# A hybrid attention and retention block: the order of two copies in a shared PSUM bank, and fewer, pinned requests

## The chip, the cores and the metric

The kernel runs on one core of a Trainium2 chip. A core has five engines that each work through a queue of their own in order: TensorE (PE, matrix products and transposes), VectorE (DVE, elementwise work and reductions), ScalarE (ACT, functions and copies), GpSimd (POOL) and SyncE (SP, which here issues all DMA requests). Data lies in DRAM, in the on-chip SBUF, or in PSUM, eight banks into which PE writes its results. The metric is the device time of one execution in microseconds (us); the kernel before took a median of 2294.67 us in three runs.

## The reference

One decoder block on an input of 1024 tokens by 1024 channels, in float32. A normalised input is projected into queries, keys and values of twelve attention heads, into retention's queries, keys, values and its gate, and into two sigmoid gates. Attention is dilated and windowed, retention is done in chunks of 128 tokens, both are projected and merged, and a squared-ReLU MLP follows:

```python
xn = rmsnorm(x, norm1_g[l])
wl = w_in[l]
qa, ka, va, qr, kr, vr, gr, gate_a, gate_b = [xn @ wl[:, bounds[i]:bounds[i + 1]] for i in range(len(IN_SPLITS))]
qa = rmsnorm(qa.reshape(B, S, ATT_HEADS, ATT_HEAD_DIM), q_norm_g[l])
ka = rmsnorm(ka.reshape(B, S, ATT_HEADS, ATT_HEAD_DIM), k_norm_g[l])
...
for gi, (window, dilation) in enumerate(ATT_GROUPS):        # (128,1), (512,4), (2048,16)
    hs = slice(gi * ATT_HEADS_PER_GROUP, (gi + 1) * ATT_HEADS_PER_GROUP)
    o, lse = dilated_group(qa[:, :, hs], ka[:, :, hs], va[:, :, hs], slopes[hs], window, dilation)
    outs.append(o)
    lses.append(lse)
alpha = jax.nn.softmax(jnp.stack(lses, axis=0), axis=0)
o_a = jnp.sum(alpha[..., None] * jnp.stack(outs, axis=0), axis=0).reshape(B, S, ATT_OUT_W).astype(x.dtype)
o_r = retention(qr, kr, vr)                                 # reshaped by heads
o_r = (head_groupnorm(o_r, ret_gn_g[l], ret_gn_b[l]) * jax.nn.silu(gr.astype(jnp.float32))).astype(x.dtype)
y = jax.nn.sigmoid(gate_a) * (o_a @ w_proj_a[l]) + jax.nn.sigmoid(gate_b) * (o_r @ w_proj_b[l])
x = x + y @ w_out[l]
xn2 = rmsnorm(x, norm2_g[l])
x = x + jnp.square(jax.nn.relu(xn2 @ w_up[l])) @ w_down[l]
```

In `dilated_group` every query block of 128 attends its own block and the one before it: scores plus a linear bias, a softmax, and the sum over the values.

## The kernel before, in words

Large products are done with each float32 operand split in a rounded high part and a rest (`split`: an ACT copy, L330, and a DVE subtraction, L333), and three matmuls (high by high, high by rest, rest by high). The input projection besides saves products in Strassen's manner: a unit of 256 output columns takes seven products (N1 to N7) of 12 large matmuls each. One such product is called a slot. `Pipe` (`pipe`) counts the slots: a function given to `pipe.at(lag, fn)` is run, and its instructions placed, among the matmuls of the slot that comes `lag` slots later; if two functions are due, the first comes after the second of four terms and the other after the third.

The stages are: attention values for all heads (results to DRAM as `v_d`); the input projection of 36 units, of which the first 12 give one head's queries and keys each (scaled roots of their squares to `rs_d`, the rest to `qk_d`, L808); retention in 32 chunks; the projection of attention's output with the first gate; that of retention's output with the second; the output projection; the MLP.

Attention has no stage of its own. Its 96 blocks (12 heads of 8 blocks, in the order of slot and group, strides 4, 8 and 1) are placed from slot 138 of the input projection on, 9 slots to a head. `plan_core` writes them as `events` per slot. With p0 the first slot of head n: `prepare` at p0 - 4 asks for the bias (L679); `bring` at p0 - 4 and at p0 asks for one half of the queries, keys and roots (L697); `scale` multiplies them on DVE two and three slots later (L705); `fetch` asks for one block's values in each slot (L711). A block's work is in `attend`: `scores` in the slot itself (PE, L642; DVE adds the bias and takes the minimum, L645; ACT takes the exponential, L647), and three slots later `turned`, which takes one PSUM bank from the ring `tr` of two. In that bank, columns 0 to 127 receive the output of the block two turns before (`values`: PE, L660; ACT copies it to `acc`, L661; a DMA writes it to DRAM, L662), and the columns behind it receive the transposed probabilities of this block (`turn`: PE, L653; ACT copies them to `pT`, L655). `scores` takes the ring's other bank. The framework makes an engine wait for another one's access to the same PSUM bank whatever the columns.

The order on PE is that of the program. On the other engines and in SP's queue a planner with a cost model places each instruction as early as it thinks its inputs are there; `tc.keep_in_program_order` pins one instruction behind everything that was written before it on its engine. Pools of tiles have a fixed number of buffers: a request or a copy into one waits until the last reader of the buffer's old content is done. `combine` mixes the three groups of a slot's heads; it reads `acc_d` (L446) some slots after the last of the three heads.

Two other places matter here. Between attention and retention, the upper half of the normalised input, kept in DRAM as `xs_d` during attention, is reloaded (L844) and retention's first chunks are asked for (`load_chunk`, L882 and L884). In the two gated projections, gates are loaded (`sg_d`) and put through a sigmoid on ACT at the place of their use (L1034, L1102).

Of the kernel before, what the change touches and what calls it, by code (L numbers as in the profile page):

```python
# [276 lines left out]
def hybrid_block(ctx: ExitStack, tc: tile.TileContext, a: dict, out: bass.AP):  # L277
# [153 lines left out]
    def tokens(rows, g, b):  # L431

        if g == 0:
            return rows[b * P:(b + 1) * P]
        if g == 1:
            return rows[512 * (b % 2):512 * (b % 2) + 512].rearrange("(p r) e -> r p e", r=4)[b // 2]
        return rows.rearrange("(p r) e -> r p e", r=8)[b]

# [186 lines left out]

    def attend(n, b, bias, qk, V, core):
# [6 lines left out]
        acc = core.tile([P, DH + 2], F, name="acc", bufs=7)  # L633

        def scores():
            sp = tr.tile([P, 4, P], F, name="tr")[:, :nk].rearrange("p a b -> p (a b)")
            q = qk[0][b // 4][:, b % 4 * P:b % 4 * P + P]
            at = 0
            for c in range((b + 1 - nk) // 4, b // 4 + 1):
                n0, n1 = max(b + 1 - nk, 4 * c), min(b + 1, 4 * c + 4)  # L640
                to = slice(at, at + (n1 - n0) * P)
                nc.tensor.matmul(sp[:, to], q, qk[1][c][:, (n0 - 4 * c) * P:(n1 - 4 * c) * P], start=True, stop=True)  # L642
                at = to.stop
            s = st["p"] = core.tile([P, 2 * P], F, name="s", bufs=3)
            nc.vector.tensor_tensor_reduce(s[:, :w], sp, bias[:, 2 * P - w:], op0=OP.add, op1=OP.min,  # L645
                                           scale=1.0, scalar=3.0e38, accum_out=acc[:, DH:DH + 1])
            nc.scalar.activation(s[:, :w], s[:, :w], AF.Exp, scale=-1.0, bias=acc[:, DH:DH + 1],  # L647
                                 accum_out=acc[:, DH + 1:DH + 2])

        def turn(bank):  # L650
            tp = bank[:, 1:]
            for j in range(nk):
                nc.tensor.transpose(tp[:, j], st["p"][:, j * P:(j + 1) * P], ident)  # L653
            st["t"] = core.tile([P, 2, P], F, name="pT", bufs=2)
            nc.scalar.activation(st["t"][:, :nk], tp[:, :nk], AF.Copy)  # L655

        def values(bank):
            po = bank[:, 0]
            for j in range(nk):
                nc.tensor.matmul(po, st["t"][:, j], V[b + 1 - nk + j], start=(j == 0), stop=(j == nk - 1))  # L660
            nc.scalar.activation(acc[:, :DH], po, AF.Copy)  # L661
            nc.sync.dma_start(tokens(acc_d[:, h, :], g, b), acc)  # L662

        return scores, turn, values

# [3 lines left out]
    def plan_core():  # L669
# [3 lines left out]
        tiles = {}  # L673

        def prepare(n):

            slot, g = heads[n]
            bias = core.tile([P, 2 * P], F, name="bias", bufs=2)
            nc.sync.dma_start(bias, a["c_bias"][g * SLOTS + slot])  # L679
            tiles[n] = bias, ([], []), {}, {}  # L680

        def bring(n, c):

            slot, g = heads[n]
            r = strides(g)
            for f in range(2):
                x = core.tile([P, 512], F, name="qk"[f] + "T", bufs=2)
                rb = core.tile([P, 512], F, name="rb", bufs=2)
                for j in range(2) if r > 1 else (c,):
                    cs = slice(256 * c, 256 * c + 256) if r > 1 else slice(0, 512)  # L690
                    src = rs_d[4 * n + 2 * f + j, cs]
                    roots = bass.AP(tensor=src.tensor, offset=src.offset, ap=[[0, P], [1, cs.stop - cs.start]])
                    for dst, src in ((x, qk_d[n, f, j][:, cs]), (rb, roots)):
                        if r > 1:
                            dst = dst.rearrange("p (r j i) -> p j r i", r=r // 2, j=2)[:, j]
                            src = src.rearrange("p (r i) -> p r i", r=r // 2)
                        nc.sync.dma_start(dst, src)  # L697
                tiles[n][1][f].append(x)
                tiles[n][2][c, f] = x, rb

        def scale(n, c, f):
            slot, g = heads[n]
            h = g * SLOTS + slot
            x, rb = tiles[n][2].pop((c, f))
            nc.vector.scalar_tensor_tensor(x, x, gqk[:, f, h:h + 1], rb, op0=OP.mult, op1=OP.mult)  # L705

        def fetch(n, b):

            slot, g = heads[n]
            V = tiles[n][3][b] = core.tile([P, DH], F, name="V", bufs=6)  # L710
            nc.sync.dma_start(V, tokens(v_d[n // 4][:, (n % 4) * DH:(n % 4) * DH + DH], g, b))  # L711

        def on(p, fn):
            events.setdefault(p, []).append(fn)

        def begin(n, b):

            bias, qk, _, V = tiles[n]
            stages.append(attend(n, b, bias, qk, V, core))

        stages = []

        def turned(m):

            bank = tr.tile([P, 4, P], F, name="tr")
            if m >= 2:
                stages[m - 2][2](bank)
            if m < len(stages):
                stages[m][1](bank)

        for n in range(HEADS):
            p0 = FIRST + EACH * n
            on(p0 - 4, lambda n=n: prepare(n))
            for c in range(2):
                on(p0 - 4 + 4 * c, lambda n=n, c=c: bring(n, c))
                for f in range(2):
                    on(p0 - 2 + 4 * c + f, lambda n=n, c=c, f=f: scale(n, c, f))
            for b in range(NT):
                p, m = p0 + b, NT * n + b
                on(p, lambda n=n, b=b: fetch(n, b))  # L740
# [6 lines left out]
        for s in range(SLOTS - 1):  # L747
            for i in range(NT // PAIR):
# [7 lines left out]
                for m in range(PAIR + 1):  # L756
                    on(p + 2 + m, lambda held=held: held["parts"].pop(0)())
                on(p + 4 + PAIR, lambda held=held: pipe.at(0, held["parts"].pop(0)))

    with ExitStack() as ph:  # L760
# [8 lines left out]
        def square(n, f, i, sg):  # L769
# [7 lines left out]
            def add():  # L777
# [8 lines left out]
                if sums["n"] == 8 * HEADS:  # L786
# [55 lines left out]
    XS[0, 1] = slot_of(pool(ctx, "x01b", 1))  # L842
    for i, x in enumerate(XS[0, 1]):
        nc.sync.dma_start(x.bitcast(F).rearrange("p a b -> p (a b)"), xs_d[i])  # L844

# [20 lines left out]
    with ExitStack() as ph:  # L866
# [153 lines left out]
    with ExitStack() as ph:  # L1020
        ES, e1, exts = None, ExitStack(), ExitStack()
        OPB = [{"N5": XS[0, 1], "N7": XS[1, 1]}, {}]
        waiting = [("N7", 1)] + [(name, h) for name in ("N1", "N2", "N6") for h in range(2)]
        for n, (d, cs) in enumerate(work):
            if not cs.start:
                ua, = W.take(1)
                uh, ul = W[ua]
            if len(gates) < len(work):
# [4 lines left out]
                           for k in range(SLOTS)], {SLOTS - 1: lambda: W.free(ua)} if cs.start else None)  # L1033
            nc.scalar.activation(gates[n], gates[n], AF.Sigmoid)  # L1034
            nc.vector.tensor_tensor(gates[n], gates[n], pp, op=OP.mult)
# [54 lines left out]
        def result(j, f, cs, src):  # L1090

            n = results.index((j, f, cs.start // 512))
            fetch(n + 2)
            if n not in ahead:
                y = src
# [5 lines left out]
            sgb, y, *pa = ahead.pop(n)  # L1101
            nc.scalar.activation(sgb, sgb, AF.Sigmoid)  # L1102
            if pa:
# [23 lines left out]
        fetch(0)  # L1127
        fetch(1)
        for i, (j, name) in enumerate(order):
            product("pb", j, name, unit, OPB[j // 4], lambda: parts, result)  # L1130
# [404 lines left out]
```

## Time and profile before

| | before |
|---|---|
| median of three runs | 2294.67 us (2290.59 to 2295.46) |
| the profiled execution | 2290.41 us |
| its span, first to last instruction | 2288.6 us |
| granted TensorE clock | 0.994 |
| PE busy | 2196.0 us, 96% |
| DVE, ACT, POOL busy | 61%, 50%, 14% |
| DMA | 359.12 MB, 157 GB/s over the span |

Busy time is the time in which an engine executes instructions. Matmuls are pipelined, so that one is listed with a longer time than the distance to the next one's start. A row of waits names the engine and line that stood idle, what released it, and total us, number of times and the longest. A row of a group or of the order of time names the line, the engine, the operation, what it writes and reads by the program's names, and the shape. A row of a stretch gives its length, then the busy time of PE, weight loads, DVE, ACT and POOL with their instruction counts, the granted clock, the DMA engines' mean share and GB/s.

### The profile page before, as it was taken

Reading aid. Unit: us, or ns where it says so; the run is one execution under the profiler, and the core shown is the slowest. Engines: PE = TensorE matmul, PEld = TensorE weight load, DVE = VectorE, ACT = ScalarE, POOL = GpSimd, SP = SyncE. Lnnn points to the kernel's source line nnn. Section 1 sums busy time; section 2 is a strip of 40 time slices with the busy share of each in tenths; the row PEclk is TensorE's granted clock in tenths of the full one; section 3 lists DMA queues with packets and bytes.
Section 4 is the critical chain, followed back from the end, with each engine's and each line's share of the span. In section 5 each row is a group of like instructions: output and inputs, shape, how many; then the busy total and the mean of one; then the engine's idle time right before and its main releaser. Section 6 shows DMA issues by size and latency. Waiting matters only on the chain. (4 is left out here: it accounts for less than half of the span.)

```text
span 2288.6 us, 29131 instructions
## 1 busy us (share of the span) xinstructions
PE 2196.0 (96%) x9928; PEld 1792.8 (78%) x9928; DVE 1389.2 (61%) x2374; ACT 1138.0 (50%) x2145; POOL 330.2 (14%) x340
## 2 busy tenths in 40 slices
PE   8999999999898889989999999999999999999999
PEld 6888888778677777778887877877778888777777
DVE  5624455655445555546776766784765556777874
ACT  4426656434544444434555555553455555754542
POOL 1000000000000000000321230000000000567883
PEclk9999999999999999999999999999999999999999
DMA  5322323433556665653554568775345556745442
GB/s 200 138 74 100 100 94 102 142 129 104 163 154 191 173 196 167 193 177 108 162 154 129 146 193 272 250 254 170 108 121 152 152 153 196 237 145 180 161 134 102
DMA packets 317367, 359.12 MB, mean 157 GB/s; under 512 B 54513, under 2 KB 230001, under 8 KB 316706
## 3 DMA queue, kind: packets, MB, share of 16 engines
q1 hardware_dynamic: 317218, 357.26, 50.3%
q8 instruction: 78, 1.28, 0.2%
q14 instruction: 71, 0.58, 0.1%
HBM read 240.59 MB, written 116.59 MB: 156 GB/s over the span
## 5 line engine op out<-in xcount | busy, mean ns | idle before, releaser
L333 DVE TENSOR_TENSOR wl<-raw,wh 128x1024 fp32r<-128x1024 f32 (+1 forms) x308 | 344.1, 1118 | 382.6 <-ACT wh L330 381.4
L330 ACT ACTIVATE wh<-raw 128x1024 fp32r<-128x1024 f32 (+1 forms) x308 | 295.5, 961 | 263.8 <-PE ms L229 92.9
L229 PE MATMUL mm<-xh,wh 128*128 128x512 f32 x960 | 389.9, 406 | 9.9 <-ACT ms L398 9.5
L229 PE MATMUL mm<-xl,wh 128*128 128x512 f32 x960 | 376.2, 392 | 0.3 <-DVE xl L333 0.3
L229 PE MATMUL mm<-xh,wl 128*128 128x512 f32 x960 | 376.4, 392 | 0.0
L229 PE MATMUL ms<-xh,wh 128*128 128x512 f32 x784 | 316.8, 404 | 3.4 <-DVE St L958 1.6
L229 PE MATMUL ms<-xh,wl 128*128 128x512 f32 x784 | 306.7, 391 | 0.0
L229 PE MATMUL ms<-xl,wh 128*128 128x512 f32 x784 | 306.5, 391 | 0.0
L229 PEld LDWEIGHTS mm<-xh,wh 128*128 128x128 f32 x960 | 183.1, 191 | 47.9 <-ACT ms L398 12.4
L229 PEld LDWEIGHTS mm<-xh,wl 128*128 128x128 f32 x960 | 181.2, 189 | 39.2
L229 PEld LDWEIGHTS mm<-xl,wh 128*128 128x128 f32 x960 | 181.6, 189 | 35.2 <-DVE xl L333 0.7
L944 POOL TENSOR_TENSOR st<-st,half 128x1 f32<-128x1 f32 x32 | 26.4, 823 | 1161.6 <-PE ms L229 1000.1
L229 PE MATMUL mm<-wh,xh 128*128 128x512 f32 x458 | 187.3, 409 | 2.5 <-ACT xh L330 2.0
L229 PE MATMUL mm<-wh,xl 128*128 128x512 f32 x458 | 180.3, 394 | 0.3 <-DVE xl L333 0.3
L229 PE MATMUL mm<-wl,xh 128*128 128x512 f32 x458 | 179.3, 392 | 0.0
L229 PEld LDWEIGHTS ms<-xh,wh 128*128 128x128 f32 x784 | 148.9, 190 | 33.7 <-DVE St L958 2.0
L229 PEld LDWEIGHTS ms<-xh,wl 128*128 128x128 f32 x784 | 147.6, 188 | 31.7
L229 PEld LDWEIGHTS ms<-xl,wh 128*128 128x128 f32 x784 | 147.8, 189 | 27.8
L645 DVE CUSTOM_DVE_ANT_0 s<-tr,bias 128x128 f32<-128x128 f32 (+1 forms) x96 | 33.6, 350 | 114.8 <-PE tr L642 114.4
L229 PEld LDWEIGHTS mm<-wh,xl 128*128 128x128 f32 x458 | 86.5, 189 | 20.2 <-DVE xl L333 0.8
L229 PEld LDWEIGHTS mm<-wh,xh 128*128 128x128 f32 x458 | 86.8, 189 | 19.2 <-ACT xh L330 2.4
L229 PEld LDWEIGHTS mm<-wl,xh 128*128 128x128 f32 x458 | 87.0, 190 | 15.8
(306 smaller groups left out, 4017.5 us busy)
## 6 DMA issues: line engine op xcount, KB each, us to landing
raw<-in_w_up SPq DMA_DIRECT2D x32, 512.0 KB, 3.8
h_d<-s SPq DMA_DIRECT2D x64, 256.0 KB, 4.3
raw<-in_w_down SPq DMA_DIRECT2D x32, 512.0 KB, 4.1
raw<-in_w_aqk_q SPq DMA_DIRECT2D x24, 512.0 KB, 3.6
qk_d<-sg SPq DMA_DIRECT2D x48, 256.0 KB, 2.5
s<-sg_d SPq DMA_DIRECT2D x40, 256.0 KB, 4.4
xh<-h_d SPq DMA_DIRECT2D x11, 896.0 KB, 4.9
s<-on_d SPq DMA_DIRECT2D x36, 256.0 KB, 5.0
```

What stands on the lines that cost most here:

```text
L229: self.nc.tensor.matmul(ps, x, y, start=start, stop=stop, skip_group_check=not first)
L330: hi = nc.scalar.activation(dst_h, src, AF.Copy)
L333: nc.vector.tensor_tensor(dst_l, src, dst_h.bitcast(F), op=OP.subtract)
L645: nc.vector.tensor_tensor_reduce(s[:, :w], sp, bias[:, 2 * P - w:], op0=OP.add, op1=OP.min, scale=1.0, scalar=3.0e38, accum_out=acc[:, DH: ...
L944: nc.gpsimd.tensor_tensor(st[:, 9:10], st[:, 8:9], half[:, 0:1], op=OP.pow)
```

## The change

Six edits are made together.

- In `turned`, the copy of the values out of the bank is written behind the transposes and their copy: `turn` and `values` are each split into a PE part and an ACT part.
- Queries and keys of a head lie side by side in DRAM (`qk_d`), already in the order of its strides; one request brings half of both, one more brings their roots. The writes at L808 put the pieces in place instead of the reads. The roots are written head by head (`hand`, from slot 98 on, two requests each) instead of once.
- Values are fetched, and results written, for two blocks at once. Buffers: bias 1 (was 2), `qk` 2 of both (was 2 each), roots 1 of both (was 2 single ones), values 4 pairs (was 6 blocks), `acc` 4 pairs (was 7 blocks).
- The requests of `prepare`, `bring` and `fetch` and the scaling are pinned; the bias is asked for at p0 - 1; the steps of `combine` come one slot later.
- The reload of `xs_d` is written behind `load_chunk(0)` and `load_chunk(1)`, pinned.
- The gates' sigmoids are pinned, each one result ahead of its use.

```diff
-    qk_d = dram.tile([HEADS, 2, 2, P, 512], F, name="qk_d")
-    rs_d = dram.tile([4 * HEADS, 512], F, name="rs_d")
+    qk_d = dram.tile([HEADS, P, 2, S], F, name="qk_d")
+    rs_d = dram.tile([HEADS, 2, S], F, name="rs_d")
...
+        def turned(bank):
             st["t"] = core.tile([P, 2, P], F, name="pT", bufs=2)
-            nc.scalar.activation(st["t"][:, :nk], tp[:, :nk], AF.Copy)
+            nc.scalar.activation(st["t"][:, :nk], bank[:, 1:1 + nk], AF.Copy)
...
-            nc.scalar.activation(acc[:, :DH], po, AF.Copy)
-            nc.sync.dma_start(tokens(acc_d[:, h, :], g, b), acc)
+        def valued(bank):
+            nc.scalar.activation(acc[:, :DH], bank[:, 0], AF.Copy)
+            if b % 2:
+                nc.sync.dma_start(tokens(acc_d[:, h, :], g, b - 1), pair)
...
+        def late(ins):
+            tc.keep_in_program_order(ins)
...
+            bias = core.tile([P, 2 * P], F, name="bias", bufs=1)
+            late(nc.sync.dma_start(bias, a["c_bias"][g * SLOTS + slot]))
...
+            x = core.tile([P, 2, 512], F, name="qk", bufs=2)
+            rb = core.tile([P, 2, 512], F, name="rb", bufs=1)
+            late(nc.sync.dma_start(x, qk_d[n, :, :, 512 * c:512 * c + 512]))
+            src = rs_d[n, 0, 512 * c:512 * c + 512]
+            late(nc.sync.dma_start(rb, bass.AP(tensor=src.tensor, offset=src.offset, ap=[[0, P], [S, 2], [1, 512]])))
...
+            late(nc.vector.scalar_tensor_tensor(x, x, gqk[:, f, h:h + 1], rb, op0=OP.mult, op1=OP.mult))
...
+            V = tiles[n][3][b // 2] = core.tile([P, 2, DH], F, name="V", bufs=4)
+            late(nc.sync.dma_start(V, tokens(v_d[n // 4][:, (n % 4) * DH:(n % 4) * DH + DH], g, b)))
...
             if m >= 2:
-                stages[m - 2][2](bank)
+                stages[m - 2][3](bank)
             if m < len(stages):
                 stages[m][1](bank)
+                stages[m][2](bank)
+            if m >= 2:
+                stages[m - 2][4](bank)
...
-            on(p0 - 4, lambda n=n: prepare(n))
+            on(p0 - 1, lambda n=n: prepare(n))
...
-                    on(p + 2 + m, lambda held=held: held["parts"].pop(0)())
-                on(p + 4 + PAIR, lambda held=held: pipe.at(0, held["parts"].pop(0)))
+                    on(p + 3 + m, lambda held=held: held["parts"].pop(0)())
+                on(p + 5 + PAIR, lambda held=held: pipe.at(0, held["parts"].pop(0)))
...
-                    nc.sync.dma_start(rs_d, root[:k])
+                    def hand(n):
+                        r = strides(heads[n][1])
+                        for f in range(2):
+                            m = 4 * n + 2 * f
+                            nc.sync.dma_start(rs_d[n, f].rearrange("(r j i) -> j r i", r=r, j=2),
+                                              root[m:m + 2].rearrange("j (r i) -> j r i", r=r))
+                    for n in range(HEADS):
+                        events.setdefault(98 + 3 * n, []).append(lambda n=n: hand(n))
...
-                nc.sync.dma_start(qk_d[j, f, i], sg)
+                to = qk_d[j, :, f].rearrange("p (r j i) -> j p r i", r=r, j=2)[i]
+                src = sg.rearrange("p (r i) -> p r i", r=r)
+                nc.sync.dma_start(to, src)
...
-    for i, x in enumerate(XS[0, 1]):
-        nc.sync.dma_start(x.bitcast(F).rearrange("p a b -> p (a b)"), xs_d[i])
...
+    def sigmoid(x):
+        tc.keep_in_program_order(nc.scalar.activation(x, x, AF.Sigmoid))
...
         load_chunk(0)
         load_chunk(1)
+        for i, x in enumerate(XS[0, 1]):
+            tc.keep_in_program_order(nc.sync.dma_start(x.bitcast(F).rearrange("p a b -> p (a b)"), xs_d[i]))
...
-            nc.scalar.activation(gates[n], gates[n], AF.Sigmoid)
+            if n < len(work) - 1:
+                sigmoid(gates[n + 1])
...
+            if n + 1 in ahead:
+                sigmoid(ahead[n + 1][0])
...
-            nc.scalar.activation(sgb, sgb, AF.Sigmoid)
```

More of the change, by code (lines that the diff above doesn't have):

```diff
@@ L433, in tokens @@
         if g == 0:
-            return rows[b * P:(b + 1) * P]
+            return rows[b * P:(b + 2) * P].rearrange("(k p) e -> p k e", k=2)
         if g == 1:
-            return rows[512 * (b % 2):512 * (b % 2) + 512].rearrange("(p r) e -> r p e", r=4)[b // 2]
-        return rows.rearrange("(p r) e -> r p e", r=8)[b]
+            return rows.rearrange("(k p r) e -> r p k e", k=2, r=4)[b // 2]
+        return rows.rearrange("(p r) e -> p r e", r=8)[:, b:b + 2]
     def has_prev(g, b):
@@ L623, in hybrid_block, with attend @@
     nc.sync.dma_start(gng, a["ret_gn"])
-    def attend(n, b, bias, qk, V, core):
+    def attend(n, b, bias, qk, V, acc, core):
         slot, g = heads[n]
@@ L632, in attend @@
         st = {}
-        acc = core.tile([P, DH + 2], F, name="acc", bufs=7)
+        pair, acc = acc, acc[:, b % 2]
         def scores():
             sp = tr.tile([P, 4, P], F, name="tr")[:, :nk].rearrange("p a b -> p (a b)")
-            q = qk[0][b // 4][:, b % 4 * P:b % 4 * P + P]
+            q = qk[b // 4][:, 0, b % 4 * P:b % 4 * P + P]
             at = 0
@@ L641, in scores @@
                 to = slice(at, at + (n1 - n0) * P)
-                nc.tensor.matmul(sp[:, to], q, qk[1][c][:, (n0 - 4 * c) * P:(n1 - 4 * c) * P], start=True, stop=True)
+                nc.tensor.matmul(sp[:, to], q, qk[c][:, 1, (n0 - 4 * c) * P:(n1 - 4 * c) * P], start=True, stop=True)
                 at = to.stop
@@ L659, in values @@
             for j in range(nk):
-                nc.tensor.matmul(po, st["t"][:, j], V[b + 1 - nk + j], start=(j == 0), stop=(j == nk - 1))
-            nc.scalar.activation(acc[:, :DH], po, AF.Copy)
-            nc.sync.dma_start(tokens(acc_d[:, h, :], g, b), acc)
-        return scores, turn, values
+                k = b + 1 - nk + j
+                nc.tensor.matmul(po, st["t"][:, j], V[k // 2][:, k % 2], start=(j == 0), stop=(j == nk - 1))
+        def valued(bank):
+            nc.scalar.activation(acc[:, :DH], bank[:, 0], AF.Copy)
+            if b % 2:
+                nc.sync.dma_start(tokens(acc_d[:, h, :], g, b - 1), pair)
+        return scores, turn, turned, values, valued
     FIRST, EACH, PAIR = 138, 9, 2
@@ L673, in plan_core @@
         tiles = {}
+        def late(ins):
+            tc.keep_in_program_order(ins)
         def prepare(n):
             slot, g = heads[n]
-            bias = core.tile([P, 2 * P], F, name="bias", bufs=2)
-            nc.sync.dma_start(bias, a["c_bias"][g * SLOTS + slot])
-            tiles[n] = bias, ([], []), {}, {}
+            bias = core.tile([P, 2 * P], F, name="bias", bufs=1)
+            late(nc.sync.dma_start(bias, a["c_bias"][g * SLOTS + slot]))
+            tiles[n][0] = bias
         def bring(n, c):
[L684 to L699, printed above, removed]
+            x = core.tile([P, 2, 512], F, name="qk", bufs=2)
[3 more added lines that the diff above has]
+            late(nc.sync.dma_start(rb, bass.AP(tensor=src.tensor, offset=src.offset, ap=[[0, P], [S, 2], [1, 512]])))
+            tiles.setdefault(n, [None, [], {}, {}])[1].append(x)
+            tiles[n][2][c] = x, rb
         def scale(n, c, f):
@@ L703, in scale @@
             h = g * SLOTS + slot
-            x, rb = tiles[n][2].pop((c, f))
-            nc.vector.scalar_tensor_tensor(x, x, gqk[:, f, h:h + 1], rb, op0=OP.mult, op1=OP.mult)
+            x, rb = (y[:, f] for y in tiles[n][2][c])
+            late(nc.vector.scalar_tensor_tensor(x, x, gqk[:, f, h:h + 1], rb, op0=OP.mult, op1=OP.mult))
         def fetch(n, b):
             slot, g = heads[n]
-            V = tiles[n][3][b] = core.tile([P, DH], F, name="V", bufs=6)
-            nc.sync.dma_start(V, tokens(v_d[n // 4][:, (n % 4) * DH:(n % 4) * DH + DH], g, b))
+            V = tiles[n][3][b // 2] = core.tile([P, 2, DH], F, name="V", bufs=4)
+            late(nc.sync.dma_start(V, tokens(v_d[n // 4][:, (n % 4) * DH:(n % 4) * DH + DH], g, b)))
         def on(p, fn):
             events.setdefault(p, []).append(fn)
+        pairs = {}
         def begin(n, b):
             bias, qk, _, V = tiles[n]
-            stages.append(attend(n, b, bias, qk, V, core))
+            if b % 2 == 0:
+                pairs[n] = core.tile([P, 2, DH + 2], F, name="acc", bufs=4)
+            stages.append(attend(n, b, bias, qk, V, pairs[n], core))
         stages = []
@@ L739, in plan_core @@
                 p, m = p0 + b, NT * n + b
-                on(p, lambda n=n, b=b: fetch(n, b))
+                if b % 2 == 0:
+                    on(p, lambda n=n, b=b: fetch(n, b))
                 on(p, lambda n=n, b=b: begin(n, b))
@@ L1023, in hybrid_block @@
         waiting = [("N7", 1)] + [(name, h) for name in ("N1", "N2", "N6") for h in range(2)]
+        sigmoid(gates[0])
         for n, (d, cs) in enumerate(work):
@@ L1128, in hybrid_block @@
         fetch(1)
+        sigmoid(ahead[0][0])
         for i, (j, name) in enumerate(order):
```

## The prediction

> **What bounds the kernel now.** I read the page first, then the waits of TensorE (PE), then the order of time around the wait that stood first, then the stage that holds it, and last what the other queues do there.
>
> ```profile
> span 2288.6 us, 29131 instructions
> PE 2196.0 (96%) x9928; PEld 1792.8 (78%) x9928; DVE 1389.2 (61%) x2374; ACT 1138.0 (50%) x2145; POOL 330.2 (14%) x340
> ```
>
> PE is the bound: it is in order, busy for 2196.0 of 2288.6 us, and nothing else comes near. So an edit is worth what it takes from, or adds to, PE's 92.6 us of gaps and the slow starts behind them. The waits of PE say where the gaps are (engine and line, what was waited for: us, times, longest):
>
> ```profile
> PE tr L653 <- ACT acc L661: 43.4, 94, 2.2
> PE mm L229 <- ACT ms L398: 9.5, 7, 2.2
> PE ms L911 <- DMA rkT<-rqk_d: 5.3, 1, 5.3
> PE ms L229 <- DVE s L1035: 1.1, 1, 1.1
> ```
>
> Nearly half is one wait. In 94 of the 96 turns of an attention block the transposes (L653) stand until ScalarE (ACT) has copied the block values (L661), because both lie in one PSUM bank. How much a turn loses is read from the order of time: first transposes with no values ahead of them, then values with no transposes behind them, then both (start us, duration, what).
>
> ```profile
> 570.05 0.39 PE L229 MATMUL ms<-xh,wl 128*128 128x512 f32 x1
> ...
> 570.28 0.38 PE L653 MATMUL tr<-ident,s 128*128 128x128 f32 x2
> ...
> 570.74 0.40 PE L229 MATMUL ms<-xl,wh 128*128 128x512 f32 x1
> ...
> 1003.38 0.40 PE L229 MATMUL ms<-xh,wl 128*128 128x512 f32 x1
> 1003.62 0.61 PE L660 MATMUL tr<-V,pT 128*128 128x128 f32 x4
> 1004.59 0.44 PE L653 MATMUL tr<-ident,s 128*128 128x128 f32 x2 [0.37 <-ACT acc L661]
> ...
> 1005.10 0.40 PE L229 MATMUL ms<-xl,wh 128*128 128x512 f32 x1
> ...
> 1006.02 0.40 PE L229 MATMUL mm<-xh,wl 128*128 128x512 f32 x1
> ...
> 1007.40 0.40 PE L229 MATMUL mm<-xh,wl 128*128 128x512 f32 x1
> 1007.64 0.61 PE L660 MATMUL tr<-V,pT 128*128 128x128 f32 x4
> ...
> 1008.31 0.40 PE L229 MATMUL mm<-xl,wh 128*128 128x512 f32 x1
> ```
>
> Large matmuls start 0.23 us apart (1006.02 to 1007.40 is six steps). From the last large one before an insert to the second one after it is two steps, 0.46, when nothing stands between. Transposes alone take it to 0.69, so they cost 0.23; values alone take it to 0.91, so 0.45; both with the wait take 1.72, so 1.26. The wait therefore costs 1.26 - 0.68 = 0.58 us, of which the trace calls 0.37 idle. The other 0.21 is PE starting again from empty, which counts as busy.
>
> The stage and its neighbours:
>
> ```profile
> 566.00:1006.00 440.00, 396.62 (x1913) 320.38 (x1912) 228.96 (x627) 211.02 (x546) 0.00 (x0) 1.00 0.60 173
> DVE s L645 <- PE tr L642: 114.2, 61, 4.2
> ACT acc L661 <- PE tr L660: 63.9, 67, 2.9
> ACT pT L655 <- PE tr L653: 44.6, 90, 0.6
> DVE qT L705 <- DMA qT<-qk_d: 12.7, 9, 2.8
> DVE kT L705 <- DMA kT<-qk_d: 6.6, 6, 2.3
> ```
>
> The first row is 440 us, then the busy times of PE, weight load, VectorE (DVE), ACT and GpSimd, then granted clock (1.00) and DMA share. DVE is at 52%, ACT at 48%, and both mostly stand waiting for PE: PE may go faster before either is the limit. With 63 us less in this stage (377) they would be at 61% and 56%.
>
> **The change part by part.**
>
> *Values' copy behind the turn.* PE now runs values, then transposes, back to back in the bank; ACT copies first the transposes, then the values. No instruction is added. What goes is 43.4 us of idle time plus 94 x 0.21 = 19.7 us of restarting: 63.1 us. What is late next: the values' copy ends later, and with it the bank, but PE wants that bank again only at the next turn, 12 large matmuls on (12 x 0.23 = 2.8 us, with scores more). The two copies are short (PE's usual wait for one was 0.37 us), and the longest lateness of ACT that PE ever met here is 2.2 us. I take no new wait; the ends are 0 and, if each turn still lost its 0.37, 35 us.
>
> *Half the requests.* Of 12 heads, 8 have a stride. Such a head asked for 1 bias, 16 pieces of q, k and roots, 8 values and 8 results, in all 33; the other four for 25: 364. Now each asks for 1 + 4 + 4 + 4 = 13: 156, and 24 small writes of the roots take the place of one. SyncE's queue (SP) spends 0.3 to 0.5 us on each, which PE does not wait for, so this alone is worth nothing on PE. It also drops waits of SP: value requests no longer stand for a buffer of six (the first row below), there being four pairs.
>
> ```profile
> SPq L711 <- PE tr L660: 68.0, 36, 6.7
> SPq L697 <- PE tr L642: 25.1, 20, 9.3
> rb<-rs_d SPq DMA_DIRECT2D x52, 128.0 KB, 3.9
> rb<-rs_d SPq DMA_DIRECT2D x16, 256.0 KB, 4.3
> qT<-qk_d SPq DMA_DIRECT2D x8, 256.0 KB, 2.8
> raw<-in_w_rqk_q SPq DMA_DIRECT2D x16, 512.0 KB, 4.4
> bias<-in_c_bias SPq DMA_DIRECT2D x10, 128.0 KB, 3.5
> ```
>
> *The pins, and fewer buffers.* This is the part that can cost. A request for q and k, and the scaling on DVE, now stand behind all that was written before them on their queue: writes of results (waiting for ACT), weight loads (waiting for DVE). Queued behind a late scaling on DVE are the scores' reduction of the next block and the weight splits, and PE waits for the former through the bank of the scores, a slot later. A slot is one product of 12 large matmuls with the scores and the turn placed in it, 440 / 106 = 4.15 us now (106 slots from the first block's turn to the last) and 377 / 106 = 3.55 after. The two requests of a chunk are 512 KB each. From the rows, 512 KB lands in 4.4 us and the roots, behind it, some 2 to 4 us after that (alone they took 4.3 where as much of q took 2.8): 6.5 to 8.5 us from issue. The scaling comes two slots after the event that asks, 7.1 us, and the request itself may leave a slot late. So I expect DVE to wait about 0 to 3 us for most of the 24 chunks (before: 15 waits, 19.3 us, longest 2.8, none of which reached PE). The slack of the scores' bank is near one slot, so most of it stays off PE. Bounds: 0, and 24 x 2.8 = 67 us if a wait as long as today's longest reached PE in full each time. I take 8 us (0.33 a chunk), nearer to the low end because today's waits reached PE in no case. The bias has one buffer and is asked for one slot before its use (3.5 us to land, and by the slot's length some 6 from the event to the first block's reduction): inside these 8. The combining of the heads is one slot later; it is on no path of PE.
>
> *The layout in DRAM.* q, k are now written in pieces of 2048, 512 or 256 bytes by stride, and read in rows of 2 KB; before, the pieces were on the read side. The writes are in a stage where PE is idle for 0.6 us of 270.
>
> ```profile
> 160.00:430.00 270.00, 269.39 (x1183) 221.59 (x1182) 137.51 (x177) 163.25 (x240) 0.00 (x0) 1.00 0.30 101
> qk_d<-sg SPq DMA_DIRECT2D x48, 256.0 KB, 2.5
> ```
>
> A write in rows lands in 2.5 us; one in 1024 pieces of 256 bytes I bound by twice the roots of 128 KB, read in pieces of 256 or 512 bytes: 7.8. There are two staging buffers, and the four results of a unit come at least a slot (2.8) apart, so a buffer must be free some 4.5 us after its write is issued. At 4 to 5 us nothing happens; at 7.8 ACT waits about 3.3 us twice a unit, in four units: 26 us at most. I take 0: even against 256 KB of q in rows (2.8), the roots in pieces (3.9) are only 1.1 us later.
>
> *First chunk ahead of the reload.*
>
> ```profile
> 1015.76 0.38 SPq L844 DMA_DIRECT2D xl<-xs_d  x1
> ...
> 1025.45 0.33 SPq L182 DMA_DIRECT2D raw<-in_w_rv  x1
> 1025.87 0.39 SPq L882 DMA_DIRECT2D rqT<-rqk_d  x1
> ...
> 1028.90 0.90 SPq L882 DMA_DIRECT2D rqT<-rqk_d  x1
> ...
> 1030.68 0.55 PE L911 MATMUL ms<-rqT,rkT 128*128 128x128 f32 x1 [5.35 <-DMA rkT<-rqk_d]
> ...
> 1012.00:1050.00 38.00, 32.65 (x149) 26.96 (x148) 15.88 (x30) 12.57 (x25) 0.55 (x1) 0.96 0.71 214
> ```
>
> The reload already goes out 10 us ahead of the first chunk and is not what the chunk waits for: it follows a weight load on SP at once. So the 5.35 us stay. The reload's 2 MB now go out behind the second chunk, ahead of the third; at the 214 GB/s that this stretch shows they take some 10 us, and the third chunk is wanted two chunks after 1030.68, each with 24 large matmuls (5.5 us): near 1041.7, some 12 us after its old request. Bounds -5.3 and +4; I take +1.
>
> ```profile
> ACT s L1102 <- DMA s<-sg_d: 19.3, 12, 3.1
> 1209.59 1.28 ACT L1034 ACT_TABLE_LOAD   x1 [3.43 <-DMA s<-sg_d]
> ```
>
> *Sigmoids pinned.* Each is issued one result ahead of its use, in its written place. ACT's 12 waits for gate loads matter only through PE's waits for ACT and DVE in these stages, at most the 9.5 + 1.1 us above. A pinned sigmoid also has one result less for its load, and the table load (1.28 us) moves from 1209.59 to the start of the projections. Bounds -9 and +5; I take -2. The Trainium skill (ScalarE: Activation LUTs, What ACT_TABLE_LOAD costs) gives 1283 ns for the load, as the trace has it, and adds a drain of about 1380 ns per switch; by it this step would be 1.4 us worse.
>
> *Sum.* 2290.4 (the profiled execution's time) - 63.1 + 8 + 0 + 1 - 2 = 2234.3. The median of the runs shown, 2294.67, is 1.0019 times the profiled run: 2238.5, so **2239 us**.
>
> **The rivals.**
>
> *Half is given back (about 2265).* The same stalls as in the 8 us, at 1.4 us a chunk (24 x 1.4 = 34). For it: DVE waits today already, the requests are larger, PE comes 14% sooner. Against it: SP loses 208 requests and 68 us of buffer waits.
>
> *Late scaling eats it all (slower, about 2318).* A pinned request stands behind a blocked weight load or result write on SP, the roots' single buffer adds the scaling before, and PE waits at each chunk. It decides from 63.1 / 24 = 2.6 us a chunk; at 3.6 it gives 24 x 3.6 = 86 us, +23 net. Against it: SP's longest waits in this stage were for buffers that the change adds to.
>
> *Slow small writes (about 2265).* The 26 us above reach PE in the head stage. The Trainium skill (DMA: Bandwidth & Descriptors, Specifications) says that below 512 bytes the engine does a read-modify-write, which speaks for this; no row here shows such a write of 256 bytes.
>
> *The wait only changes place (about 2290).* ACT's copies come late in its queue, and PE waits at the next turn for the bank as long as now. Against it: ACT waited for PE at 90 of 96 of L655's copies.
>
> *More than the sum (about 2224).* No stall at the chunks, and the sigmoids give all they can.
>
> **How the numbers follow.** Forecast 0.62; half back 0.15; small writes 0.05; late scaling 0.10; same place 0.03; more 0.05. About 0.2% (4.6 us) is what a measurement of this kernel can tell from no change. Faster: 0.62 + 0.15 + 0.05 + 0.05 = 0.87; same 0.03; slower 0.10. The forecast's own range is 2226 to 2252; the whole range goes from 2222, just under the case without any new wait, to 2270, which takes in both cases of 2265.
>
> **What would show it.** Right: PE's wait of L653 for ACT is gone or under 3 us, the stage from the first turn to the last is about 385 us instead of 440, and L705's waits on DMA stay under 50 us. Wrong: a new wait of PE on DVE (scores, L645) or on ACT for the turn's bank; PE idle in the stage of the heads behind ACT L806; a longer wait at the third chunk. If all these are absent and the time is still high, a stage far from the change was ordered anew.

## The result, and the profile after

The changed kernel took a median of 2228.18 us (2224.38 to 2229.98) where the kernel before took 2292.63 (2286.51 to 2295.46): a ratio of 0.972, 95% interval 0.9695 to 0.9745. The forecast was 2239 us, 2222 to 2270. The profiled execution took 2229.98 us at a granted clock of 0.996 (before: 2290.41 us at 0.994).

The page and the waits of PE after:

```profile
span 2228.2 us, 28853 instructions
PE 2174.8 (98%) x9928; PEld 1785.4 (80%) x9928; DVE 1390.9 (62%) x2374; ACT 1127.4 (51%) x2145; POOL 330.5 (15%) x340
...
PE mm L229 <- ACT ms L398: 9.7, 8, 2.5
PE tr L1192 <- DVE x L1212: 5.9, 1, 5.9
...
PE tr L642 <- DVE qk L705: 3.5, 4, 1.9
PE ms L933 <- DMA rkT<-rqk_d: 3.5, 1, 3.5
...
PE ms L229 <- DVE s L1059: 1.6, 2, 1.2
...
PE tr L663 <- ACT acc L666: 1.2, 1, 1.2
```

The row of 43.4 us, L653 behind ACT, is gone. The place of the old wait now looks like this in PE's order of time:

```profile
950.72 0.40 PE L229 MATMUL ms<-xh,wl 128*128 128x512 f32 x1
950.95 0.61 PE L663 MATMUL tr<-V,pT 128*128 128x128 f32 x4
951.40 0.38 PE L653 MATMUL tr<-ident,s 128*128 128x128 f32 x2
951.53 0.48 PE L229 MATMUL ms<-xh,wh 128*128 128x512 f32 x1
951.86 0.39 PE L229 MATMUL ms<-xl,wh 128*128 128x512 f32 x1
```

From the last large matmul (950.72) to the second one after the turn (951.86) is 1.14 us, less two steps of 0.23: values and transposes together cost 0.68 us, which is the sum of the two alone (0.45 and 0.23) and 0.58 less than before. PE's busy time also fell, by 21.2 us, though it executes the same 9928 matmuls. Of this, 17.4 us lie in the attention stage, and the last section says why; the other 3.8 go with the granted clock, 0.996 in place of 0.994.

Where the time went can be cut at four points that both programs have: the first and the last transposes of a turn (L653), the first transposes of retention's output, and the first transposes of the MLP's input. The rows of the last three in both kernels give first and last start (before, then after):

```profile
L653 PE MATMUL tr<-ident,s x140: 272/328/333, 567.0 to 1004.8; 128*128 128x128 f32 x140
L971 PE MATMUL tr<-ident,on x128: 270/272/328, 1046.8 to 1356.5; 128*128 128x128 f32 x128
L1166 PE MATMUL tr<-ident,xn x64: 270/272/446, 1612.4 to 1665.4; 128*128 128x128 f32 x64
```

```profile
L653 PE MATMUL tr<-ident,s x140: 271/273/273, 566.4 to 951.5; 128*128 128x128 f32 x140
L993 PE MATMUL tr<-ident,on x128: 269/272/300, 991.8 to 1298.2; 128*128 128x128 f32 x128
L1192 PE MATMUL tr<-ident,xn x64: 270/272/449, 1553.4 to 1606.4; 128*128 128x128 f32 x64
```

| stretch | before | after | difference |
|---|---|---|---|
| to the first turn | 567.0 | 566.4 | -0.6 |
| first to last turn (the attention stage) | 437.8 | 385.1 | -52.7 |
| to retention's first output | 42.0 | 40.3 | -1.7 |
| to the MLP's first input | 565.6 | 561.6 | -4.0 |
| to the end | 676.2 | 674.8 | -1.4 |
| span | 2288.6 | 2228.2 | -60.4 |

So seven eighths of the gain is in the one stage. (Of the 4.0 us up to the MLP's input, 2.1 are PE's busy time there, 549.76 us before and 547.68 after, at a granted clock of 0.99 and 1.00.) There 10.4 us of the 63.1 that the wait was reckoned at are missing; PE's waits inside that stage, 566.4 to 951.5, are new ones:

```profile
PE tr L642 <- DVE qk L705: 2.8, 3, 1.9
PE mm L229 <- ACT ms L398: 2.2, 2, 1.4
PE tr L663 <- ACT acc L666: 1.2, 1, 1.2
PE tr L642 <- issue: 0.9, 1, 0.9
PE ms L229 <- ACT u L406: 0.9, 1, 0.9
```

They are 8.0 us; with a restart of 0.21 us, as the prediction read it, at each of the 8 they come to 9.7.

### The profile page after: what moved, and what is told of

It is laid out like the page before. It is cut to its first block, busy times and chain, and to the rows that moved or that the text cites. A ratio compares the mean times of both kernels' runs of the same rounds, so it can differ in the third digit from the quotient of the medians.

```text
span 2228.2 us, 28853 instructions
## 1 busy us (share of the span) xinstructions
PE 2174.8 (98%) x9928; PEld 1785.4 (80%) x9928; DVE 1390.9 (62%) x2374; ACT 1127.4 (51%) x2145; POOL 330.5 (15%) x340
## 5 line engine op out<-in xcount | busy, mean ns | idle before, releaser
L229 PE MATMUL mm<-xl,wh 128*128 128x512 f32 x960 | 376.0, 392 | 0.3 <-DVE xl L333 0.3
L229 PEld LDWEIGHTS mm<-wh,xl 128*128 128x128 f32 x458 | 86.6, 189 | 20.2 <-DVE xl L333 0.8
L1392 DVE TENSOR_TENSOR Y<-Y,ms 128x512 f32<-128x512 f32 x88 | 59.7, 682 | 55.6 <-PE ms L229 55.5
```

What stands on the lines that cost most here:

```text
L229: self.nc.tensor.matmul(ps, x, y, start=start, stop=stop, skip_group_check=not first)
L1392: nc.vector.tensor_tensor(Y[r][:, ns], Y[r][:, ns], ps, op=op)
```

## The experiments

The theory after this reading (A): the order in the bank is the whole gain, and the new requests take back some 10 us of it. The rival (B): the requests and pins carry a share, or make the gain possible. "Stage" below is always the time from the first to the last start of the turns' transposes (L653) in that run's profile, and each ratio is to the kernel before as it was timed beside that run (medians of 2287.60 to 2288.99 us).

**The order alone.** To the kernel before, only this:

```diff
             if m >= 2:
-                stages[m - 2][2](bank)
+                stages[m - 2][3](bank)
             if m < len(stages):
                 stages[m][1](bank)
+                stages[m][2](bank)
+            if m >= 2:
+                stages[m - 2][4](bank)
```

> The kernel before with the new order of the two copies alone (values' copy behind the next turn's transposes and their copy); requests, pins, reload and sigmoids as before. Theory A (the wait in the bank is nearly the whole gain, 63 us less what new waits give back): 50 to 63 us faster than before, ratio 0.973 to 0.978, no wait of PE at L653, the time from the first turn's transposes to the last near 380 us. Theory B (the requests and pins are needed, because with PE 12% faster in this stage the old 364 requests keep SP and DVE too late): at most 35 us faster, ratio 0.985 or more, with new waits of PE on DVE (scaling or scores) in their place.

Measured: 2224.86 us, ratio 0.9721 (0.9703 to 0.9739), as much as the six edits together. The row of its turns' transposes (first and last start), and all of PE's waits between them:

```profile
L653 PE MATMUL tr<-ident,s x140: 272/273/273, 566.6 to 941.7; 128*128 128x128 f32 x140
```

```profile
PE tr L662 <- ACT acc L665: 0.3, 1, 0.3
PE tr L642 <- DVE acc L645: 0.2, 1, 0.2
PE ms L229 <- ACT u L406: 0.2, 1, 0.2
```

The stage is 375.1 us, 62.7 less than before, with 0.7 us of waits left. B falls: the 364 old requests keep up with the faster PE.

**The order undone.** The changed kernel, with the values' copy put back ahead of the turn:

```diff
                 stages[m - 2][3](bank)
+                stages[m - 2][4](bank)
             if m < len(stages):
                 stages[m][1](bank)
                 stages[m][2](bank)
-            if m >= 2:
-                stages[m - 2][4](bank)
```

> The changed kernel with only the copies' order put back (values' copy ahead of the turn). Theory A: within 6 us of before (ratio 0.997 to 1.002), PE's wait at L653 back at 40 to 50 us. Theory B (requests and pins carry a share of their own): 10 to 30 us faster than before, ratio 0.987 to 0.996.

Measured: 2286.55 us, ratio 0.9996 (0.9983 to 1.0008). The wait is back:

```profile
PE tr L653 <- ACT acc L666: 45.8, 94, 2.4
```

The stage is 445.2 us, 7.4 longer than before. The other five edits together are worth nothing in time, and in this stage they cost.

**All but the new requests.** The kernel before with the order, the reload and the sigmoids of the change, but the old requests for the heads, not pinned. It was measured twice, the second time on one chip with the changed kernel and a version that also lacks the sigmoids:

```diff
             if m < len(stages):
                 stages[m][1](bank)
+                stages[m][2](bank)
+            if m >= 2:
+                stages[m - 2][4](bank)
...
         load_chunk(1)
+        for i, x in enumerate(XS[0, 1]):
+            tc.keep_in_program_order(nc.sync.dma_start(x.bitcast(F).rearrange("p a b -> p (a b)"), xs_d[i]))
...
-            nc.scalar.activation(gates[n], gates[n], AF.Sigmoid)
+            if n < len(work) - 1:
+                sigmoid(gates[n + 1])
```

> The kernel before with the new order, the reload behind the first chunks and the pinned sigmoids, but the old 364 unpinned requests for the heads. Theory A: within 5 us of the changed kernel (ratio 0.970 to 0.976). Theory B: 15 us or more slower than the changed kernel (ratio 0.979 or more).

> The new order, the reload and the sigmoids with the old requests, beside the changed kernel on the same chip. If the requests' part costs: 5 to 9 us faster than the changed kernel. If not: within 3 us of it. Against the version without the sigmoids: within 3 us if they are worth nothing.

> The changed kernel itself, so that it stands on the same chip as the others of this call: ratio 0.971 to 0.974 by the first measurement. If its distance to the version without the new requests vanishes here, that distance was the chip's and not the requests'.

> The kernel before with the new order and the reload behind the first chunks, nothing else: the two parts that the runs so far show to help. If the sigmoids are worth nothing and the requests' part costs 5 to 9 us net: 5 to 9 us faster than the changed kernel beside it, ratio to before 0.968 to 0.9705. If the requests' cost in their stage is given back later: within 3 us of the changed kernel.

| kernel | median, us | ratio to before (95%) | stage, us |
|---|---|---|---|
| order, reload, sigmoids (first time) | 2220.80 | 0.9696 (0.9675 to 0.9718) | 376.1 |
| order, reload, sigmoids (second time) | 2220.52 | 0.9701 (0.9684 to 0.9718) | 374.9 |
| order, reload (second time) | 2225.72 | 0.9722 (0.9706 to 0.9738) | 376.0 |
| changed kernel (second time) | 2229.14 | 0.9741 (0.9725 to 0.9756) | 385.0 |

The version in the first two rows beats the changed kernel by 8.6 us on the same chip, with intervals that don't meet, and is the fastest one measured. At first it was expected within 5 us of the changed kernel, which was too near; the second expectation, 5 to 9 us faster, is met. The stage says where: 385.1 and 385.0 with the new requests, 374.9 to 376.1 in the four runs with the old ones (the order alone among them).

The version without the sigmoids was expected to be as fast as the one with them, and 5 to 9 us faster than the changed kernel or else within 3. It lies 5.2 us above the one and 3.4 below the other, between its cases, with intervals that overlap both. The 5.2 us can't be put down to the sigmoids: in the two profiles, the stretch from retention's first output to the MLP's first input takes 568.1 us without them and 563.4 with them, but 3.6 of these 4.7 us are PE's busy time (551.19 and 547.60), at a granted clock of 0.99 and 1.00. About 1 us of waiting is left, and what the sigmoids add beside the others is not settled.

**The pins.**

```diff
         def late(ins):
-            tc.keep_in_program_order(ins)
+            return ins
```

> The changed kernel with the requests of the heads and the scaling not pinned (the planner places them), all else kept. Theory A (the pins are neutral; what is left of PE's waits in the stage, some 8 us, comes from late roots for the scaling): within 5 us of the changed kernel, ratio to before 0.970 to 0.975, DVE still waits for the roots 20 to 40 us. Rival (the pins hold the requests to the point of their use and their loss would let scaling wait on other things, or without them the requests go out earlier): 8 us or more to either side, ratio under 0.969 or over 0.976.

Measured: 2226.15 us, 0.9722 (0.9702 to 0.9742), not told apart from the changed kernel by time. The stage is 380.8 us, 4.3 less. By one profile of this version, the pins are thus a little under half of the stage's loss. DVE's waits did not stay as expected: it stands 1.2 us for the roots, and for the queries and keys themselves instead:

```profile
DVE qk L705 <- DMA qk<-qk_d: 38.2, 17, 5.2
```

Yet PE no longer waits behind the scaling at all in the stage (2.8 us with the pins).

**Requests a slot later, a slot earlier, and split.** Three edits of `bring` in the changed kernel test whether the loss comes from DVE's scaling standing for the roots (32.2 us, 17 times, after the change):

First, all requests a slot later:

```diff
-                on(p0 - 4 + 4 * c, lambda n=n, c=c: bring(n, c))
+                on(p0 - 3 + 4 * c, lambda n=n, c=c: bring(n, c))
```

> The changed kernel with each request for queries, keys and roots one slot later (3.6 us), the scaling where it was: it doubles the suspected cost. If DVE's waits for the roots pass to PE in full beyond today's, 24 x 3.6 = 86 us are lost and the ratio to before is about 1.01 (the rival of late scaling, as far as its mechanism goes). If a slot of slack in the scores' bank takes most of it, as I hold, DVE waits 80 to 120 us for the roots and PE loses 10 to 45 us: ratio 0.976 to 0.992.

Second, the second half of a head a slot earlier:

```diff
-                on(p0 - 4 + 4 * c, lambda n=n, c=c: bring(n, c))
+                on(p0 - 4 + 3 * c, lambda n=n, c=c: bring(n, c))
```

> The changed kernel with the second half of each head's queries, keys and roots asked for one slot earlier (its buffer is free by then). If the late roots cause PE's 4 us of waits at the scores: DVE's waits for the roots fall by a third or more and the kernel gains 1 to 4 us on the changed one (ratio to before 0.970 to 0.972). If not, no difference.

Third, each request split in two, with two single buffers for the roots:

```diff
-            rb = core.tile([P, 2, 512], F, name="rb", bufs=1)
-            late(nc.sync.dma_start(x, qk_d[n, :, :, 512 * c:512 * c + 512]))
+            rbs = []
+            for f in range(2):
+                late(nc.sync.dma_start(x[:, f], qk_d[n, :, f, 512 * c:512 * c + 512]))
+                rbs.append(core.tile([P, 512], F, name="rb", bufs=2))
+                src = rs_d[n, f, 512 * c:512 * c + 512]
+                late(nc.sync.dma_start(rbs[f], bass.AP(tensor=src.tensor, offset=src.offset, ap=[[0, P], [1, 512]])))
```

> The changed kernel with each chunk's request for q and k, and that for their roots, split in two (q, its root, k, its root) and two single buffers for the roots, in the same memory; pins kept. If PE's loss in the stage comes from the scaling standing for the larger requests and their one buffer: DVE's waits for the roots fall to half or less and the stage from the first turn to the last to 378 to 382 us (385.1 in the changed kernel), 3 to 7 us faster than it. If the number of requests matters more: no gain or slower.

The waits of DVE's scaling for a DMA over the whole execution (us, times, longest), in this order: the changed kernel, a slot later, a slot earlier, split.

```profile
DVE qk L705 <- DMA rb<-rs_d: 32.2, 17, 3.4
```

```profile
DVE qk L705 <- DMA rb<-rs_d: 41.5, 20, 5.8
```

```profile
DVE qk L705 <- DMA rb<-rs_d: 21.3, 13, 3.1
```

```profile
DVE qk L707 <- DMA rb<-rs_d: 25.8, 14, 3.8
```

The stages are 385.1, 385.8, 383.1 and 385.6 us, the ratios 0.972, 0.9764 (0.9749 to 0.9779), 0.9726 (0.9713 to 0.974) and 0.9746 (0.9732 to 0.976). For the slot later I had expected 80 to 120 us of waits and a loss of 10 us or more; it was 9 us more waiting, 0.7 us in the stage, and some 4 to 5 us by the medians (2233.38 against 2228.18 and 2229.14), so that only its ratio is just inside what I expected. The slot earlier took a third of the waiting away and 2 us of the stage; by time it is not told apart from the changed kernel. The split took away a fifth, not the half that it was meant to, and nothing of the stage. None of the three moved the waiting far, so by themselves they show only that PE meets a small part of DVE's waits. Two other runs say that they are not the whole: with the order undone DVE stood only 3.7 us for the roots in the stage, which was 7.4 us longer even so, and the pins' run above had more waiting of DVE and a shorter stage.

The trace of the changed kernel says more about its 8.0 us. In the three waits behind the scaling (2.8 us) the scaling itself had waited for no DMA; DVE came to it late from the work written before it. But two others, behind ACT's L406 and L398 (0.86 us each), do go back to the roots. This is the first of them:

```profile
691.70 0.75 DVE L705 SCALAR_TENSOR_TENSOR qk<-qk,gqk,rb 128x512 f32<-128x512 f32 x1 [1.89 <-DMA rb<-rs_d]
...
693.27 0.40 ACT L647 ACTIVATE s<-s,acc 128x128 f32<-128x128 f32 x1 [1.94 <-DVE acc L645]
...
694.30 0.50 PE L229 MATMUL ms<-xh,wh 128*128 128x512 f32 x1 [0.86 <-ACT u L406]
```

DVE stands for the roots, the reduction of the scores (L645) comes late behind the scaling, ACT's exponential (L647) stands for it, and ACT's next work, for which PE waits, comes late in its turn. The wait behind the values' copy (1.2 us) has the same start: DVE stood 2.75 us for roots until 630.34 and split a weight after that, SP stood 3.9 us for that split before it could ask for the next weight, at 632.25, and ACT stood 2.15 us for this weight with the copies queued behind it. So at least 3.0 of the 8.0 us go back to late roots. Another 2.8 stand behind the scaling without such a wait of its own, 1.35 behind a weight that ACT (L398) got 6.8 us after its request, and 0.9 the profile does not attribute.

What differs besides is SP's queue. In the stage it waits like this in the changed kernel and in the one with the order alone:

```profile
SPq L668 <- ACT acc L666: 42.1, 27, 4.2
SPq L182 <- DVE wl L333: 40.3, 16, 7.1
SPq L842 <- DVE u L412: 30.6, 14, 4.2
SPq L842 <- ACT sg L840: 24.4, 16, 3.9
SPq L688 <- DVE acc L645: 16.5, 5, 6.1
```

```profile
SPq L666 <- ACT acc L665: 49.6, 52, 3.9
...
SPq L182 <- DVE wl L333: 10.7, 5, 4.2
SPq L701 <- PE tr L642: 10.0, 2, 9.4
SPq L830 <- ACT sg L828: 9.4, 14, 1.7
```

Weight loads (L182) and writes of results (L842 behind sg; L830 in the other) stand 3.8 and 2.6 times as long, and the queue now also stands at the bias (L688). That goes with a queue in which more is held in written order. But no run takes these waits away one by one: beyond the pins' 4.3 us, what in the requests' part (their size, the fewer buffers, the later steps of `combine`, the order that the planner then finds) costs the other 5 us stays open.

**The reload alone.** In the kernel before:

```diff
-    for i, x in enumerate(XS[0, 1]):
-        nc.sync.dma_start(x.bitcast(F).rearrange("p a b -> p (a b)"), xs_d[i])
...
         load_chunk(1)
+        for i, x in enumerate(XS[0, 1]):
+            tc.keep_in_program_order(nc.sync.dma_start(x.bitcast(F).rearrange("p a b -> p (a b)"), xs_d[i]))
```

> The kernel before with the reload of the normalised input behind the first two chunk requests, pinned, alone. The prediction's step: +1 us (bounds -5.3 and +4), PE still waits 5.35 us for the first chunk. The rival, from the changed kernel's trace, where the first chunk was asked for 5 us before its use: the first chunk's wait goes and another at the second chunk takes its place, net -1 to -4 us, ratio 0.998 to 0.9995.

Measured: 0.9988 (0.9978 to 0.9999), by this ratio 2.7 us faster (0.2 to 5.0), by the medians 1.0 (2286.57 against 2287.60): a gain at the edge of the noise, where its rival had it. In the changed kernel's order of time the first request of the first chunk on SP, and the scores of the first two chunks on PE, are:

```profile
967.14 0.37 SPq L902 DMA_DIRECT2D rqT<-rqk_d  x1
...
971.97 0.61 PE L933 MATMUL ms<-rqT,rkT 128*128 128x128 f32 x4
...
978.38 0.69 PE L933 MATMUL ms<-rqT,rkT 128*128 128x128 f32 x4 [3.48 <-DMA rkT<-rqk_d]
```

The first chunk no longer waits; the second does, 3.48 us (3.6 in the run of the reload alone) in place of 5.35.

**The sigmoids alone.** In the kernel before, with `sigmoid` the pinned activation of the change:

```diff
-            nc.scalar.activation(gates[n], gates[n], AF.Sigmoid)
+            if n < len(work) - 1:
+                sigmoid(gates[n + 1])
...
+            if n + 1 in ahead:
+                sigmoid(ahead[n + 1][0])
...
-            nc.scalar.activation(sgb, sgb, AF.Sigmoid)
```

> The kernel before with the pinned, earlier sigmoids alone. The prediction's step: -2 us (bounds -9 and +5). Rival: no difference, since ACT's waits for gate loads stay off PE, whose waits for ACT's L398 come from other instructions ahead of it; ratio 0.9985 to 1.001, PE's waits in the two projections unchanged within 2 us.

Measured: 1.0004 (0.9991 to 1.0016), which is 2.1 us faster to 3.7 slower. ACT still stands for gates in the two projections, 12.2 us in 9 times for the sigmoids, and PE's waits for ACT and DVE there are 8.8 us, before 9.5. No difference is seen, as the rival had it; the 2 us of the forecast lie just inside the interval.

## Why the prediction was right

*The copy behind the turn: right, to 0.4 us.* Forecast 63.1 us, of which 43.4 is listed as idle and 94 x 0.21 was read off as restarting. The order alone shortened the stage by 62.7. The restart so measures (62.7 - 43.4) / 94 = 0.205 us, or 0.22 if the three small new waits of that run (0.7 us) are counted. The Trainium skill (TensorE: Matmul & The Clock Gate, Single matmul latency) gives a single bf16 matmul at full clock a constant of 166 ns on top of the time of its columns. What is measured here lies 0.04 us or more above that, and no run shows that it is the same thing.

*No new wait at the bank: right.* 1.2 us once, 0.3 with the order alone.

*Half the requests worth nothing on PE, pins and fewer buffers +8: the size was right, and its mechanism for a part.* The stage lost 9 to 10 us and is 385.1 long, where about 385 was forecast. I had put the loss on DVE's scaling, held in written order and standing for the roots, and had it pass to PE through the scores' bank. DVE did stand for the roots (32.2 us), and in the trace at least 3.0 of PE's 8.0 us go back to that; but they came by ACT's queue and a late weight, not by the bank, and another 2.8 stand behind the scaling where it had waited for no DMA. A slot of added lateness moved the stage by 0.7 us, and splitting the requests by 0.5. The pins are 4.3 us, the rest is open, so that 8 met 9 to 10 is in part luck. The rival of late scaling, whose price was 2.6 us a chunk, falls: the stage's whole loss is 0.4 us a chunk. The Trainium skill (DMA: Bandwidth & Descriptors, Bandwidth) advises fewer, larger transfers; no run here measures its bandwidth, and in this stage 208 requests fewer brought no time: with the old requests and the new order only 0.7 us of PE's waits were left to gain.

*The layout in DRAM at 0: right.* In the stage from 160 to 430 us PE was busy for 268.67 of 270 us, before for 269.39, and the stretch to the first turn is no longer. ACT waits for the staging buffers 5.5 us in all, before 4.3. Of the rule on writes below 512 bytes in the Trainium skill (DMA: Bandwidth & Descriptors, Specifications) no more than this shows.

*The first chunk: the step "so the 5.35 us stay" failed.* That the reload was out 10 us before told only that it was not in the way on the queue, not that the planner would place the chunk's request where it had been. With the reload written behind, the first request leaves at 967.14, 4.8 us before its use at 971.97. Why the planner then places it earlier is not shown. What I had at +1 measured -2.7 alone, with an interval from -5.0 to -0.2.

*Sigmoids at -2: not shown.* Alone they measure +0.9 us, between -2.1 and +3.7. The bound of 9.5 + 1.1 us was also read too wide: the 9.5 is the row of the whole execution, and 6.1 of it lie in the two projections.

The sum thus held because its one large term did. Of the forecast's 10.8 us of error, 4.3 are the sum's own (2234.3 against 2229.98 of the profiled execution), 4.2 came from scaling it up to a median, 0.5 from rounding, and 1.8 is the changed kernel's median lying below its profiled execution.

## What to carry to other kernels

With a framework that makes engines wait for each other by the PSUM bank, as this one does (43.4 us of waits in 94 turns), write all of PE's work in a shared bank first and let the readers follow; here that is one moved copy and 2.7% of a kernel that was 96% busy. Price a wait of PE not by its idle time but from the last full-rate instruction before it to the second after it: the restart was a third of the gain and is listed as busy. And test bundled edits one by one: here one of six gave as much as all of them, and the part with most lines of code, the requests, cost 9 us.

## What the runs showed of the hardware

A gap of 0.37 us in PE's listed work cost 0.58 us of time. The rows say where the rest is: the values' matmuls are listed from 950.95 for 0.61 us, to 951.56, and the transposes start at 951.40, so in a stream 0.16 us of a matmul's listed time lies under the next one. Behind a wait it lies under nothing, and the transposes themselves are listed with a median of 328 ns, against 273 without the wait. That is 0.16 + 0.06 us, times 94 about 20.7. PE's busy time in the stage, before and with the order alone, fell by 20.2 us with the same matmuls (the second figure of each row):

```profile
567.00:1004.80 437.80, 394.42 (x1905) 318.62 (x1903) 227.47 (x625) 209.40 (x543) 0.00 (x0) 1.00 0.61 173
566.60:941.70 375.10, 374.25 (x1904) 313.71 (x1903) 224.04 (x623) 198.43 (x542) 0.00 (x0) 1.00 0.71 202
```

So "busy" held a fifth of a microsecond of stall for each wait.
